# SSD mixer: transposed b in c b's bank, other places for a gate's three norms, three tiles in the first chunk of groups with 18, one tile in front of the first decays

## The chip, the cores and the metric

The kernel runs on one core of a Trainium2 chip. Its time is the device time of one execution in microseconds (us), the median of several runs. Before the change it is 2992.21 us (three runs, 2991.93 to 2997.83). Engines: PE multiplies matrices, DVE, ACT and POOL work on vectors, SP issues DMA transfers. Each takes its instructions in order and waits at an instruction until the work of other engines that it needs is done. Matmul results land in PSUM, memory of eight banks that PE writes and DVE and ACT read; everything else lies in SBUF.

## The reference, cut to what is touched

Two layers on 1040 tokens (16 meta tokens and 1024) of width 1024: a Mamba-2 mixer (SSD) with a gated convolution FFN, then stick-breaking attention with a second FFN. The change touches only the mixer, whose mathematics for each group of 8 heads is:

```python
z, xbc, dt_raw = jnp.split(u @ w_in, [SSM_D_INNER, SSM_D_INNER + SSM_CONV_DIM], axis=-1)
xbc = jax.nn.silu(_causal_dwconv(xbc, conv_w, conv_b))
xs, b_in, c_in = jnp.split(xbc, [SSM_D_INNER, SSM_D_INNER + G * N], axis=-1)
...
cb = jnp.einsum('bclgn,bcsgn->bgcls', c_c, b_c)
y_diag = jnp.einsum('bgcls,bgecls,bcsgep->bclgep', cb, decay_in, xdt)
chunk_states = jnp.einsum('bclgn,bgecl,bclgep->cbgepn', b_c, decay_to_end, xdt)
...
hg = (y * jax.nn.silu(z.astype(f32))).reshape(b, L, G, SSM_D_INNER // G)
hg = hg * lax.rsqrt(jnp.mean(hg * hg, axis=-1, keepdims=True) + NORM_EPS)
```

So each group has a projection with convolution and silu (x, B and C), a scan over chunks of tokens, a gate z, and a norm of the gated rows over the group's 512 channels.

## The kernel before

**Tiles.** Everything is kept transposed, channels on partitions, tokens along the row. A projected *tile* is 128 channels times a third of the tokens (348, 348, 344; the list TT). Each product is made of three matmuls in float32 halves (mm3, L171 to L173) over 8 blocks of the inner dimension, so 24 matmuls of one pass each per tile, into a PSUM bank `pj`.

**Streams of tiles.** `in_group(g)` makes 18 tiles: four rows of x, one of B, one of C, three thirds each. A tile is followed by its convolution (ACT L293, three operations of DVE L296) and, when the next tile is through, by a silu (ACT L484). `gate_group(g)` makes 12 tiles of z: silu (ACT L516), product with x (DVE L523), and, in `settle()` of the *next* tile, the square (ACT L528), which DVE adds to the third's accumulator (L532, L534). When a third has its four squares, `gate_norm(g, j)` can run: `rstd` loads an ACT table (L195), sums over partitions with a matmul by ones into a bank `ms` (PE L204), takes Ln and Exp on ACT (L207, L208), four steps on DVE (L209 to L212), then four products of DVE (L545) with the rows. `stream(blocks)` hands out all tiles one by one, in the order into(1), gate(0), into(2), gate(1), into(3), gate(2), gate(3). A block without a source stands for three calls (the norms), placed between tiles: in front of the second, third and fourth tile after the gate's last one, that is offsets 1, 2 and 3.

**Chunks.** The scan takes each group in 9 chunks of 116 tokens (the last 112; the list CH). A chunk has three parts. `ssd_decays`: SP fetches the cumulated decays, broadcast (D, L587, and E, L593), DVE subtracts (eight times, L598), ACT takes the exponential (L599), POOL multiplies E by C (L602). `ssd_front`: on PE the product cb (L614), four transpositions of x into px (L617), the transposed B into pb (L627); on DVE cb masked (cbm, L620), x times dt (xdt, L622), the decays times cbm (L623); ACT copies pb to bk (L629), POOL scales xdt to xde (L631). `ssd_back`: on PE the chunk's state S from bk and xde (L644), and y from the decays and the old state (L656, L658, 16 matmuls); POOL and DVE update the state (L650, L651), DVE adds y into x (L660, four times).

**What sets the order.** On PE, DVE, ACT and POOL the mixer's instructions stand in the order in which the program writes them. Between a chunk's front and its back stand tiles taken from the stream of the *next* groups, so that PE has work while DVE, ACT and POOL prepare S and y. The numbers of tiles that groups 0 to 3 spread over their chunks are (18, 30, 30, 18): two per chunk with 18, and 4, 3, 3 in turn with 30. The decays of the next chunk are issued to SP behind the first of a chunk's tiles, and their subtraction and exponential behind the second.

**Banks.** cb, pb, y and ms take turns in three PSUM banks (`sm`); px and S have two (`lg`); tiles have two for the first two thirds (`mm`) and one for the last (`ex`). A bank is free again when its readers are done.

Of the kernel before, what the change touches and what calls it, by code (L numbers as in the profile page):

```python
# [10 lines left out]
AF = mybir.ActivationFunctionType  # L11
ALU = mybir.AluOpType

P = 128
# [72 lines left out]
class Trunk:  # L87
# [465 lines left out]
    def stream(self, blocks, w0=None):  # L553


        calls = {}
        todo = []
        for src, f in blocks:
            if src is None:
                for j in range(3):  # L560
                    calls[3 * len(todo) + 1 + j] = lambda f=f, j=j: f(j)
            else:
                todo.append((src, f))
        w = [w0 or self.load_w(todo[0][0], D)]
        for n in range(3 * len(todo)):
            i, j = divmod(n, 3)
            if j == 0:
                if i + 1 < len(todo):
                    w.append(self.load_w(todo[i + 1][0], D))
                cur = w.pop(0)  # L570
            if n in calls:
                calls.pop(n)()
            todo[i][1](cur, j)
            yield
        self.settle()
        for f in calls.values():
            f()
# [27 lines left out]
    def ssd_front(self, g, x, bt, ct, c, dk, pool):  # L605

        nc = self.nc
        h0 = GH * g
        tt = nc.vector.tensor_tensor
        t0, n = CH[c]  # L610
        cc = 3 * (c % 3) + c // 3
        e = t0 + n
        pcb = self.sm("cb")
        nc.tensor.matmul(pcb[:n, :n], bt[:, t0:e], ct[:, t0:e], start=True, stop=True)  # L614
        px = self.lg("px")
        for q in range(4):
            nc.tensor.transpose(px[:n, q * P : q * P + P], x[q][:, t0:e], self.ident)  # L617
        px = px[:n].rearrange("p (h d) -> p h d", h=GH)
        cbm = pool.tile([P, CB], F32, tag="cbm", name=self.nm("cbm"), bufs=2)
        tt(cbm[:n, :n], pcb[:n, :n], self.past[:n, :n], op=ALU.mult)  # L620
        xdt = pool.tile([P, GH, 64], F32, tag="xdt", name=self.nm("xdt"), bufs=2)
        tt(xdt[:n], px, self.cols[:n, 0, cc, h0 : h0 + GH].unsqueeze(2).to_broadcast([n, GH, 64]), op=ALU.mult)  # L622
        tt(dk, dk, cbm[:n, :n].unsqueeze(1).to_broadcast([n, GH, n]), op=ALU.mult)  # L623
        bk = xde = None
        if c < 8:
            pb = self.sm("pb")
            nc.tensor.transpose(pb[:n, :P], bt[:, t0:e], self.ident)  # L627
            bk = pool.tile([P, P], F32, tag="bk", name=self.nm("bk"), bufs=2)
            nc.scalar.activation(bk[:n], pb[:n, :P], AF.Copy)  # L629
            xde = pool.tile([P, GH, 64], F32, tag="xde", name=self.nm("xde"), bufs=2)  # L630
            nc.gpsimd.tensor_tensor(xde[:n], xdt[:n], self.cols[:n, 2, cc, h0 : h0 + GH].unsqueeze(2).to_broadcast([n, GH, 64]), op=ALU.mult)  # L631
        return xdt, xde, bk
# [31 lines left out]
    def mixer(self, mx):  # L664
# [5 lines left out]
        with self.tc.tile_pool(name="ssd", bufs=3) as pool:  # L670
            yd, rows = [None] * 4, [[] for _ in range(4)]
            accs = [{} for _ in range(4)]
# [8 lines left out]
            def gate(g):  # L681
                def norm(j):
                    self.gate_norm(g, rows[g], accs[g], j)
                    if j == 2 and g < 2:
                        yd[g] = self.spill(rows[g][:4], f"y{g}_d")
                return self.gate_group(u, g, rows[g], accs[g], later if g == 3 else lambda j, f: f()) + [(None, norm)]

            into = lambda g: self.in_group(u, g, rows[g])
            blocks = into(1) + gate(0) + into(2) + gate(1) + into(3) + gate(2) + gate(3)
# [7 lines left out]
            with self.tc.manual_schedule(engines={E.PE, E.DVE, E.Activation, E.Pool}):  # L697
                ahead = self.ssd_decays(0, rows[0][5], 0, pool)
                dk, ce = next(ahead)
                for g in range(GROUPS):  # L700
                    *x, bt, ct = rows[g]
                    tiles, given = (18, 30, 30, 18)[g], 0
                    state = None
                    for c in range(9):
                        for _ in ahead:
                            pass
                        ops = self.ssd_front(g, x, bt, ct, c, dk, pool)
                        now = dk, ce
                        for _ in range((tiles * (c + 1) + 8) // 9 - given):
                            next(work)  # L710
                            if given == (tiles * c + 8) // 9:
                                nxt = (g, ct, c + 1) if c < 8 else (g + 1, rows[g + 1][5], 0) if g < 3 else None
                                ahead = self.ssd_decays(*nxt, pool) if nxt else iter([(None, None)])
                                dk, ce = next(ahead)
                            else:
                                next(ahead, None)
                            given += 1
                        state = self.ssd_back(g, x, c, *now, *ops, state, pool)
                        if g == 3:
                            done.append(c)  # L720
                            todo, waiting[:] = waiting[:], []
                            for w in todo:
                                later(*w)
# [909 lines left out]
```

## Time and profile before

| | us |
|---|---|
| median of three runs | 2992.21 |
| the profiled execution | 2995.8 |
| its span, first to last instruction | 2994.1 |
| mean granted clock of PE in it | 0.983 |
| PE busy from 285 to 380 us (group 1's last six chunks, two norms among them) | 89.07 of 95 |
| PE busy from 440 to 540 us (the same in group 2) | 94.10 of 100 |
| PE busy from 620 to 760 us (group 3's end, what follows) | 129.30 of 140 |

A line of the timeline or of a line's instructions reads: start in us, duration in us, engine, line of the program, operation, output, inputs, shapes, how many in a row, and in brackets the idle time of the engine just before with what ended it. A duration of several instructions in a row is that of all of them. PE's matmuls are pipelined, so that one tile's 24 matmuls start some 0.16 us apart though each is shown with 0.3 us. The window row of the profile lists start and end, its length, then for PE, the weight load, DVE, ACT and POOL the busy time with the number of instructions, then the granted clock, the share of the DMA engines, and GB/s.

### The profile page before, as it was taken

The page shows a single profiled execution, that of the slowest core. Times are in us where ns is not written, and L with a number is a line of the kernel's source. Part 1 is how long each engine was busy: PE and PEld are TensorE (multiplying, and loading weights), DVE is VectorE, ACT ScalarE, POOL GpSimd, SP SyncE. Part 2 cuts the span into 40 slices and gives each one's busy share as a digit, 9 for nine tenths or more (in the row PEclk, how much of TensorE's full clock was granted, in tenths as well). Part 3 has the DMA queues.
Part 4 walks back from the last instruction along what each step waited for, and adds up shares of the span by engine and source line. Part 5 has one row for each costly group of instructions (what it writes and reads, how often), then busy time and mean ns, then how long its engine had stood idle before and what let it go on. Part 6 is the DMA issues. An engine that isn't in the chain of part 4 may idle for free.

```text
span 2994.1 us, 57318 instructions
## 1 busy us (share of the span) xinstructions
PE 2879.0 (96%) x21863; PEld 2738.0 (91%) x21863; DVE 2304.0 (77%) x4026; ACT 1653.4 (55%) x3403; POOL 1308.0 (44%) x1250
## 2 busy tenths in 40 slices
PE   7999999989998999999999999999899999999998
PEld 4999898879998999998999999999798999998878
DVE  5586868885369887878876888888839878878785
ACT  4555555553245555555334788887736555554433
POOL 1254444442334666663442222222342766764451
PEclk9999999999999999999999999999999999999999
DMA  5233333323122222224232122221331222225321
GB/s 162 70 107 90 106 89 105 106 70 139 63 80 72 79 73 84 79 86 177 74 130 86 55 61 66 64 70 54 106 141 57 80 84 78 75 82 176 106 99 64
DMA packets 123411, 272.72 MB, mean 91 GB/s; under 512 B 13664, under 2 KB 53216, under 8 KB 123136
## 3 DMA queue, kind: packets, MB, share of 16 engines
q1 hardware_dynamic: 117760, 257.93, 26.6%
q10 hardware_dynamic: 4112, 6.56, 0.7%
q0 software_dynamic: 1264, 4.57, 0.4%
q8 instruction: 172, 2.82, 0.4%
q14 instruction: 103, 0.84, 0.1%
HBM read 200.89 MB, written 53.20 MB: 85 GB/s over the span
## 4 chain that ended last, share of the span: by engine, by line
PE 77%; DVE 12%; issue 4%; ACT 3%; POOL 2%; DMA 2%; SPq 0%; DVEq 0%; ACTq 0%; POOLq 0%
PE p L172 9%; PE p L171 9%; PE p L173 9%; PE acc L172 6%; PE acc L171 6%; PE acc L173 6%; PE pj L171 6%; PE pj L172 6%; PE pj L173 6%; PE po L1366 3%; PE lg L1325 3%; PE wT L1352 2%; DVE D L598 1%; PE ms L831 1%; DVE xbc L545 1%
## 5 line engine op out<-in xcount | busy, mean ns | idle before, releaser
L171 PE MATMUL pj<-uh,wh 128*128 128x348 f32 (+2 forms) x1536 | 507.0, 330 | 11.7 <-ACT bk L629 5.9
L172 PE MATMUL pj<-ul,wh 128*128 128x348 f32 (+2 forms) x1536 | 499.7, 325 | 0.0
L173 PE MATMUL pj<-uh,wl 128*128 128x348 f32 (+2 forms) x1536 | 496.3, 323 | 0.0
L171 PE MATMUL p<-bh,fh 128*128 128x262 f32 (+1 forms) x1408 | 403.5, 287 | 7.7 <-ACT c L293 2.8
L173 PE MATMUL p<-bh,fl 128*128 128x262 f32 (+1 forms) x1408 | 402.6, 286 | 3.6 <-POOL fl L905 3.6
L172 PE MATMUL p<-bl,fh 128*128 128x262 f32 (+1 forms) x1408 | 402.3, 286 | 0.1
L905 POOL TENSOR_TENSOR fl<-x,fh 128x1024 fp32r<-128x1024 f32 x88 | 212.4, 2414 | 267.4 <-ACT fh L904 217.7
L172 PE MATMUL p<-bl,wh 128*128 128x262 f32 (+1 forms) x1056 | 302.0, 286 | 6.1 <-DVE bl L857 6.1
L171 PEld LDWEIGHTS pj<-uh,wh 128*128 128x128 f32 x1536 | 292.8, 191 | 16.2 <-ACT xbc L293 4.3
L171 PE MATMUL p<-bh,wh 128*128 128x262 f32 (+1 forms) x1056 | 302.8, 287 | 0.9 <-ACT bh L856 0.9
L173 PE MATMUL p<-bh,wl 128*128 128x262 f32 (+1 forms) x1056 | 301.9, 286 | 0.0
L165 POOL TENSOR_TENSOR wl<-w,wh 128x1024 fp32r<-128x1024 f32 (+2 forms) x76 | 155.7, 2050 | 318.7 <-ACT wh L164 318.7
L172 PEld LDWEIGHTS pj<-ul,wh 128*128 128x128 f32 x1536 | 293.2, 191 | 1.8 <-issue 1.0
L173 PEld LDWEIGHTS pj<-uh,wl 128*128 128x128 f32 x1536 | 292.7, 191 | 0.8 <-issue 0.8
L296 DVE SCALAR_TENSOR_TENSOR c<-p,params,c 128x260 f32<-128x260 f32 (+1 forms) x528 | 249.8, 481 | 54.6 <-ACT c L293 45.1
L171 PEld LDWEIGHTS p<-bh,fh 128*128 128x128 f32 x1408 | 270.2, 192 | 8.6 <-ACT c L293 6.0
L173 PEld LDWEIGHTS p<-bh,fl 128*128 128x128 f32 x1408 | 269.4, 192 | 4.1 <-POOL fl L905 4.0
L172 PEld LDWEIGHTS p<-bl,fh 128*128 128x128 f32 x1408 | 270.2, 192 | 0.6 <-DVE bl L857 0.5
L947 DVE TENSOR_TENSOR c<-c,c 128x260 f32<-128x260 f32 (+1 forms) x176 | 245.0, 1394 | 5.5 <-ACT c L943 2.4
L952 ACT ACTIVATE ft<-p 128x262 f32<-128x262 f32 (+1 forms) x352 | 127.4, 384 | 203.8 <-DVE p L955 177.0
L1055 POOL TENSOR_TENSOR wl<-w,wh 128x1024 fp32r<-128x1024 f32 x56 | 148.9, 2662 | 205.4 <-ACT wh L1054 195.7
L171 PE MATMUL acc<-gh,wh 128*128 128x260 f32 (+1 forms) x672 | 215.0, 323 | 10.9 <-DVE h L1105 7.2
(325 smaller groups left out, 8472.7 us busy)
## 6 DMA issues: line engine op xcount, KB each, us to landing
w<-in_w_up SPq DMA_DIRECT2D x88, 512.0 KB
w<-in_w_down SPq DMA_DIRECT2D x44, 512.0 KB
w<-in_w_in SPq DMA_DIRECT2D x40, 512.0 KB
E<-ea_d SPq DMA_DIRECT2D x32, 464.0 KB
D<-acs_d SPq DMA_DIRECT2D x32, 420.5 KB
g<-c SPq DMA_DIRECT2D x88, 130.0 KB
g<-c SPq DMA_DIRECT2D x88, 128.0 KB
b<-g SPq DMA_DIRECT2D x16, 520.0 KB
```

The costliest lines, as they stand in the source:

```text
L165: nc.gpsimd.tensor_tensor(wl[:, :n], w32[:, :n], wh[:, :n].bitcast(F32), op=ALU.subtract)
L171: mm(out, wh, uh, start=first, stop=False, skip_group_check=joins)
L172: mm(out, wh, ul, start=False, stop=False, skip_group_check=joins)
L173: mm(out, wl, uh, start=False, stop=last, skip_group_check=joins)
L296: nc.vector.scalar_tensor_tensor(out, ps[:, o + i : o + i + n], wcol(i), out, op0=ALU.mult, op1=ALU.add)
L905: tt(lo[:, :n], t, hi[:, :n].bitcast(F32), op=ALU.subtract)
L947: self.last_up = tt(g[:, :FN], g[:, :FN], v[:, :FN], op=ALU.mult)
L952: nc.scalar.activation(s[:, :N], ps[:, :N], AF.Copy)
L1055: pt(wl, y, wh.bitcast(F32), op=SUB)
L1325: nc.tensor.matmul(ps[:nt, :m], part[:, c0 : c0 + nt], ks[a][:, s0 : s0 + m], start=x == 0, stop=x == 1)
L1352: nc.tensor.transpose(pt[:ns, x * CB : x * CB + nt], bt[a][:nt, x * CB : x * CB + ns], self.ident[:nt, :nt])
L1366: nc.tensor.matmul(po[64 * a : 64 * a + 64, :nt], v[: CH[c][1], c, 64 * a : 64 * a + 64], wt[a][: CH[c][1], c, :nt], start=x == 0, stop=x ...
```

## The change

Four things. (1) The transposed B goes to columns 128 to 255 of cb's bank, and is made ahead of cb; pb and its bank are gone. (2) The three norms of the gates of groups 0, 1 and 2 stand at the offsets -1, 1 and 3 from the gate's end instead of 1, 2 and 3: the first in front of the gate's last tile, the second where the first stood, the third where it was. Group 3's gate keeps 1, 2, 3. (3) In groups with 18 tiles the first chunk takes three tiles, and the others two up to the last, which takes one. (4) One tile is taken from the stream ahead of group 0's first decays; it counts as the first of that chunk's three. A flag `begun` takes the place of the old test for the next chunk's decays.

```diff
@@ stream
-            if src is None:
+            if isinstance(src, tuple):
                 for j in range(3):
-                    calls[3 * len(todo) + 1 + j] = lambda f=f, j=j: f(j)
+                    calls[3 * len(todo) + src[j]] = lambda f=f, j=j: f(j)
@@ ssd_front
         pcb = self.sm("cb")
+        if c < 8:
+            nc.tensor.transpose(pcb[:n, P : 2 * P], bt[:, t0:e], self.ident)
         nc.tensor.matmul(pcb[:n, :n], bt[:, t0:e], ct[:, t0:e], start=True, stop=True)
...
-            pb = self.sm("pb")
-            nc.tensor.transpose(pb[:n, :P], bt[:, t0:e], self.ident)
             bk = pool.tile([P, P], F32, tag="bk", name=self.nm("bk"), bufs=2)
-            nc.scalar.activation(bk[:n], pb[:n, :P], AF.Copy)
+            nc.scalar.activation(bk[:n], pcb[:n, P : 2 * P], AF.Copy)
@@ mixer
-                return self.gate_group(u, g, rows[g], accs[g], later if g == 3 else lambda j, f: f()) + [(None, norm)]
+                return self.gate_group(u, g, rows[g], accs[g], later if g == 3 else lambda j, f: f()) + [((-1, 1, 3) if g < 3 else (1, 2, 3), norm)]
...
                     for c in range(9):
+                        if g == c == 0:
+                            next(work)
+                            given = 1
                         for _ in ahead:
                             pass
+                        begun = False
                         ops = self.ssd_front(g, x, bt, ct, c, dk, pool)
                         now = dk, ce
-                        for _ in range((tiles * (c + 1) + 8) // 9 - given):
+                        for _ in range(min(tiles, (tiles * (c + 1) + 8) // 9 + (tiles == 18)) - given):
                             next(work)
-                            if given == (tiles * c + 8) // 9:
+                            if not begun:
+                                begun = True
                                 nxt = (g, ct, c + 1) if c < 8 else (g + 1, rows[g + 1][5], 0) if g < 3 else None
                                 ahead = self.ssd_decays(*nxt, pool) if nxt else iter([(None, None)])
                                 dk, ce = next(ahead)
```

In the changed program the lines from L614 to L625 have moved by one or two (cb is L616, its transposition L615, cbm L622, xdt L624, the product with cbm L625); L629, L644 and the others named above are the same.

PE around the first norm of the gate in group 1's chunks: `pj` are tiles, `ms` the norms' banks, `wh` and `wl` the halves of a weight block; what stands in brackets are the engines waited for. Before, the gate's last tile (344 tokens) follows the one ahead of it, and the first norm comes after a first tile of 352 columns:

```order
L173 MATMUL pj_2770<-uh_149,wl_2538 128x348
L171 MATMUL pj_2804<-uh_135,wh_2537 128x344 [waits Activation_49]
...
L173 MATMUL pj_2850<-uh_149,wl_2692 128x352
L204 MATMUL ms_2883<-z_2316,ones 128x348 [waits DVE_49]
L171 MATMUL pj_2896<-uh_135,wh_2691 128x352 [waits Activation_49]
```

and now:

```order
L173 MATMUL pj_2758<-uh_149,wl_2528 128x348
L204 MATMUL ms_2793<-z_2307,ones 128x348 [waits DVE_49]
L171 MATMUL pj_2806<-uh_135,wh_2527 128x344 [waits Activation_49]
...
L204 MATMUL ms_2885<-z_2340,ones 128x348 [waits DVE_49,PE_49]
L171 MATMUL pj_2898<-uh_135,wh_2680 128x352 [waits Activation_49]
```

The first norm's ms (of z_2307 now, z_2316 before: the same accumulator) stands ahead of the tile of 344 tokens, and where it stood is the second norm's.

DVE at the same place, now: `xbc_888` is a row of x that the gate multiplies, `z` a tile of the gate or its square, `cbm`, `xdt` and `D` those of the next chunk's front.

```order
L523 TENSOR_TENSOR xbc_888<-xbc_888,z_2709 128x348
L651 TENSOR_TENSOR state_2717<-state_2717,S_2715 128x512 [waits PE_49,Pool_49]
L660 SCALAR_TENSOR_TENSOR xbc_1184<-xbc_1184,params,y_2720 128x116 [waits PE_49]
...
L622 TENSOR_TENSOR cbm_2749<-cb_2741,past 116x116 [waits PE_49]
L624 TENSOR_TENSOR xdt_2751<-px_2744,cols 116x512 [waits PE_49]
L625 TENSOR_TENSOR D_2635<-D_2635,cbm_2749 116x928 [waits DVE_49]
L534 TENSOR_TENSOR z_2307<-z_2307,z_2709 128x348 [waits Activation_49]
L523 TENSOR_TENSOR xbc_888<-xbc_888,z_2783 128x348
L209 TENSOR_TENSOR z_2307<-y_2795 128x348 [waits PE_49,Activation_49]
```

The last addition to the first norm's accumulator (L534) stands behind the state, the four sums with y and the front of the next chunk, as it did before; the norm's own DVE steps (from L209) now follow two rows behind it.

ACT there, before (`bk` is the copy of the transposed B):

```order
L629 ACTIVATE bk_2766<-pb_2764 116x128 [waits PE_49]
L516 ACTIVATE z_2795<-pj_2770 128x348 [waits PE_49]
L528 ACTIVATE z_2720<-xbc_888 128x348 [waits DVE_49,Activation_49]
L516 ACTIVATE z_2829<-pj_2804 128x344 [waits PE_49]
```

and now:

```order
L629 ACTIVATE bk_2754<-cb_2741 116x128 [waits DVE_49]
L516 ACTIVATE z_2783<-pj_2758 128x348 [waits PE_49]
L528 ACTIVATE z_2709<-xbc_888 128x348 [waits Activation_49]
L195 ACT_TABLE_LOAD
L207 ACTIVATE y_2795<-ms_2793 128x348 [waits PE_49]
```

bk reads cb's bank and waits for DVE, which reads cb there, instead of PE.

DVE at the first decays, before:

```order
L296 SCALAR_TENSOR_TENSOR xbc_888<-pj_919,params,xbc_888 128x348 x3
L598 TENSOR_SCALAR D_1176<-D_1176,cols 116x116 x8
L296 SCALAR_TENSOR_TENSOR xbc_888<-pj_949,params,xbc_888 128x344 x3
L296 SCALAR_TENSOR_TENSOR xbc_985<-pj_986,params,xbc_985 128x348 x3
```

and now:

```order
L296 SCALAR_TENSOR_TENSOR xbc_1082<-pj_1143,params,xbc_1082 128x344 x3
L296 SCALAR_TENSOR_TENSOR xbc_1184<-pj_1185,params,xbc_1184 128x348 x3
L598 TENSOR_SCALAR D_1176<-D_1176,cols 116x116 x8
L622 TENSOR_TENSOR cbm_1231<-cb_1223,past 116x116
L624 TENSOR_TENSOR xdt_1233<-px_1226,cols 116x512
L625 TENSOR_TENSOR D_1176<-D_1176,cbm_1231 116x928
```

The convolutions of group 0's last tiles (xbc_888, xbc_985, xbc_1082) and of one tile of group 1 (xbc_1184) now stand ahead of the first decays' subtractions.

## The prediction

> **What bounds the kernel now.** I read the page first: its busy line, then the chain of waits by engine.
>
> ```profile
> PE 2879.0 (96%) x21863; PEld 2738.0 (91%) x21863; DVE 2304.0 (77%) x4026; ACT 1653.4 (55%) x3403; POOL 1308.0 (44%) x1250
> ...
> PE 77%; DVE 12%; issue 4%; ACT 3%; POOL 2%; DMA 2%; SPq 0%; DVEq 0%; ACTq 0%; POOLq 0%
> ```
>
> PE has work for 96% of the span, and the change neither adds nor removes a matmul (of the other engines' work only two table loads of ACT go, by the order). It can only give or take idle time of PE, and what the granted clock does behind it. All that it moves lies in the mixer, so the second view is PE's waits from 100 to 760 us (waiting work, releaser: us in all, times, longest):
>
> ```profile
> PE pb L627 <- DVE z L210: 6.8, 3, 2.6
> PE ms L204 <- ACT bk L629: 6.6, 3, 5.8
> PE pj L171 <- ACT bk L629: 5.9, 2, 3.0
> PE pj L171 <- DVE xbc L296: 4.0, 1, 4.0
> PE S L644 <- POOL xde L631: 3.0, 2, 2.3
> PE y L656 <- DVE D L623: 1.5, 1, 1.5
> ```
>
> They make 27.8 us, 0.9% of the program, and each row belongs to a part of the change: the first three stand around the gates' norms (pb waits for a bank that a norm still reads; bk, queued on ACT, then holds up what is behind it), the fourth at the first decays, the fifth at the first chunk of group 3, the sixth at its last. So the sum is small, and what counts is which waits come in their place.
>
> **1. A tile in front of the first decays.** From the timeline:
>
> ```profile
> 116.99 1.61 DVE L598 TENSOR_SCALAR D<-D,cols 116x116 f32<-116x116 f32 x8 [8.86 <-DMA D<-acs_d]
> 120.45 0.63 PE L171 MATMUL pj<-uh,wh 128*128 128x348 f32 x1 [4.03 <-DVE xbc L296]
> 120.88 0.49 PE L172 MATMUL pj<-ul,wh 128*128 128x348 f32 x1
> 121.17 0.49 PE L173 MATMUL pj<-uh,wl 128*128 128x348 f32 x1
> ...
> 125.50 0.32 PE L173 MATMUL pj<-uh,wl 128*128 128x348 f32 x1
> 125.66 0.32 PE L171 MATMUL pj<-uh,wh 128*128 128x348 f32 x1
> ```
>
> DVE works in order: L598 waits 8.86 us for the decays' DMA, the convs of finished tiles stand behind it, their PSUM banks stay taken, and PE stops for 4.03 us. Behind the stop the matmuls start 0.29 us apart (120.88 to 121.17) instead of 0.16 (125.50 to 125.66), for some 17 of them: 17 x 0.13 = 2.2 us. In the change the convs of group 0's last tiles and of one tile more are queued ahead of L598, so the banks come free while the DMA is under way. I take all of it, **-6.2 us**; the other end is nothing, where a later stage was short of time anyway (rival 3).
>
> **2. One tile instead of two in group 0's last chunk.** The nearest rows are those of the chunk before it:
>
> ```profile
> 216.30 0.46 PE L614 MATMUL cb<-xbc,xbc 128*116 128x116 f32 x2
> ...
> 220.37 1.11 DVE L623 TENSOR_TENSOR D<-D,cbm 116x928 f32<-116x928 f32 x1
> ...
> 227.42 3.88 DVE L598 TENSOR_SCALAR D<-D,cols 112x112 f32<-112x112 f32 x8
> ```
>
> y needs the product of the decays with cbm, which is done 220.37 + 1.11 - 216.30 = 5.2 us after cb starts. PE has the transpositions behind cb (about 0.7) and one tile, 24 matmuls x 0.16 = 3.8, so it is there at 4.5: **+0.7 us**. It is nothing if DVE comes sooner, and up to +4 if the subtractions of the last decays (3.88 us there) come in front and the clock falls behind the wait; the regular chunk is nearest, so 0.7.
>
> **3. Groups 1 and 2: norms at -1, 1 and 3, pb in cb's bank.** What the old places cost is read from the rows of S, one per chunk:
>
> ```profile
> 302.09 1.02 PE L644 MATMUL S<-xde,bk 116*128 116x512 f32 x2
> 323.34 1.02 PE L644 MATMUL S<-xde,bk 116*128 116x512 f32 x2
> 337.78 0.63 PE L171 MATMUL pj<-uh,wh 128*128 128x352 f32 x1 [3.01 <-ACT bk L629]
> 344.49 1.02 PE L644 MATMUL S<-xde,bk 116*128 116x512 f32 x2
> 363.47 1.02 PE L644 MATMUL S<-xde,bk 116*128 116x512 f32 x2
> 378.63 1.02 PE L644 MATMUL S<-xde,bk 116*128 116x512 f32 x2
> ...
> 459.75 1.02 PE L644 MATMUL S<-xde,bk 116*128 116x512 f32 x2
> 480.98 1.02 PE L644 MATMUL S<-xde,bk 116*128 116x512 f32 x2
> 499.55 1.13 PE L644 MATMUL S<-xde,bk 116*128 116x512 f32 x2
> ```
>
> An undisturbed chunk of three tiles takes 378.63 - 363.47 = 15.16, one of four 363.47 - 344.49 = 18.98; a tile is the difference, 3.82. In group 1 the two chunks with the norms have three tiles each and take 21.25 and 21.15: 21.25 - 15.16 less two ms pairs at 0.32 is 5.45, 21.15 - 15.16 is 5.99, together **11.4 us**. In group 2 the same two take 21.23 and 18.57: 5.43 + 3.41 = **8.8 us**. Of this I let all go: pb has no bank of its own to wait for, and the four products behind each norm (L545) no longer fall in the same chunk for two norms. The other end, that it all stays, is rival 2.
>
> What comes in its place: the first norm's ms now stands on PE in front of the gate's last tile, and its input gets its last square from the tile only two before, which ACT does behind the silu of the tile just finished, and which DVE adds behind everything that it has queued. Where the last tile starts in group 1 (290.05), the trace has these rows:
>
> ```profile
> 288.08 0.27 ACT L629 ACTIVATE bk<-pb 116x128 f32<-116x128 f32 x1
> 290.05 0.32 PE L171 MATMUL pj<-uh,wh 128*128 128x344 f32 x1
> 290.25 0.46 ACT L516 ACTIVATE z<-pj 128x348 f32<-128x348 f32 x1 [1.90 <-PE pj L173]
> 291.40 0.50 ACT L528 ACTIVATE z<-xbc 128x348 f32<-128x348 f32 x1 [0.69 <-DVE xbc L523]
> 292.24 0.69 DVE L651 TENSOR_TENSOR state<-state,S 128x512 f32<-128x512 f32 x1 [0.94 <-POOL state L650]
> 293.83 0.27 DVE L620 TENSOR_TENSOR cbm<-cb,past 116x116 f32<-116x116 f32 x1
> 294.61 1.12 DVE L623 TENSOR_TENSOR D<-D,cbm 116x928 f32<-116x928 f32 x1
> 295.64 1.37 DVE L534 TENSOR_TENSOR z<-z,z 128x348 f32<-128x348 f32 x1
> 297.64 0.75 PE L204 MATMUL ms<-z,ones 128*128 128x348 f32 x2
> ```
>
> The square is done at 291.9, but the add (L534) stands behind state, four sums of x, cbm, xdt and the product with cbm, and ends at 297.0. PE, in order, would stand still from 290.05 to 297.0, 7.0 us, with the last tile queued behind ms. The stop's clock: 2.2 us was lost behind the stop of 4.03, and at 337.78 the chunk's excess of 5.99 less the wait of 3.01 leaves 3.0; I take 2.5. With 0.5 for what arrives late afterwards that is 10.0 per gate: **-1.4 us** in group 1, **+1.2** in group 2, **-0.2** together. The least it can be is ACT's and DVE's own chain, 0.46 + 0.50 + 0.52 (an uncontended add) and gaps, some 2 us, if DVE's queue is empty (rival 1). The second norm stands where the first stood and its input is then one tile older than it needs, so it stops nothing.
>
> [...]
>
> Sharing a bank has its own price: bk (ACT) now waits until DVE has read cbm, at 293.83 + 0.27 = 294.1, where it ran at 288.08, and on ACT the silu of the tile just finished and the square stand behind it. Here that ends at 294.1 + 0.27 + 0.46 + 0.50 = 295.3, still ahead of the add at 295.64, so I cost it at nothing; in other chunks DVE's part of the held-up tile stands behind the product with cbm as well. Without that cover S, a tile of 3.82 or more behind, would wait for bk by at most 294.1 - 288.1 - 3.8 = 2.2 us per chunk.
>
> [...]
>
> **4. Group 3.** The third tile in the first chunk covers the wait of S there; what binds afterwards is POOL's and DVE's turn per chunk.
>
> ```profile
> 561.87 1.62 PE L644 MATMUL S<-xde,bk 116*128 116x512 f32 x2 [2.27 <-POOL xde L631]
> 569.17 1.79 POOL L631 TENSOR_TENSOR xde<-xdt,cols 116x512 f32<-116x512 f32 x1 [2.94 <-DVE xdt L622]
> 617.29 1.85 POOL L631 TENSOR_TENSOR xde<-xdt,cols 116x512 f32<-116x512 f32 x1 [4.34 <-DVE xdt L622]
> 642.58 1.53 PE L204 MATMUL ms<-z,ones 128*128 128x348 f32 x2 [5.83 <-ACT bk L629]
> ...
> 618.20:666.40 48.20, 38.48 (x276) 33.87 (x274) 41.71 (x85) 28.05 (x38) 22.38 (x12) 0.89 0.17 52
> ```
>
> From 569.17 to 617.29 four chunks take 48.12, 12.03 each, while PE needs 15.16 - 3.82 = 11.3 for two tiles. So PE gets ahead of DVE again, and the 2.27 comes back as later waits; between 0 and 2.3 us gain. From 618.2 to the last y DVE is busy 41.71 of 48.20 us (third number group of the window), with the same instructions after the change. At most 6.5 us can go there, the wait of 5.83 at 642.58 among it; against it stands a stop at the first norm as in groups 1 and 2. I take **0**, with -3 and +3 as ends.
>
> **Sum.** -6.2 + 0.7 - 0.2 + 0 = -5.7 us, against the profiled execution's 2995.8 us (span 2994.1 and 1.7 around it): 2990.1. That execution lies 3.6 us above the median of the runs shown, 2992.21, and the same step from the median gives 2986.5; I say 2986. The ends of the terms (±3 for group 3, +3 for part 2, ±2 for each gate's stop) make its own range 2982 to 2991.
>
> **Rivals.**
> 1. The first norm hardly stops PE, because DVE's queue is shorter there once the pile is gone. Then a stop of 2 us without loss of clock leaves 11.4 - 2.4 = 9.0 and 8.8 - 2.2 = 6.6, and the total is -5.7 + 0.2 - 15.6 = -21, **2971 us**. For it: the square is done at 291.9 and POOL's state, which delays DVE at 292.24, might come earlier. Against it: all of the chunk's front is ahead of L534 in DVE's order.
> 2. Slower. The stop comes on top of the old waits, in all three gates: DVE is behind by as much as the norm's own work, the pile is only moved by one tile, and the wait of bk for cbm takes the place of that of pb for its bank. Only pb's wait for its bank, 6.8 / 3 = 2.3 us per gate, is sure to go: 7.0 - 2.3 = +4.7 for each gate, +14.1 for three, less 5.5 for parts 1 and 2: +8.6, **3001 us**. The kernel is slower than before from 1.9 us per gate above what I have, 5.7 / 3. For it: pb's waits show that DVE is the late one. Against it: the second norm is a tile further from the third.
> 3. The gain of the first decays is eaten before the group ends: S(0) then waits for xde, since the subtractions come behind three convs. Then -1 in all, **2991 us**. Against it: the chunks of group 0 show no waits of PE afterwards.
>
> **Numbers.** The forecast has 0.55, rival 1 0.15, rival 2 0.18, rival 3 0.12. 0.2% is 6.0 us, about what a measurement of this kernel can tell from no change, so faster ends at 2986.2 and slower begins at 2998.2. The forecast lies on the first bound: half of it, 0.27, and rival 1 make faster 0.42. Of rival 2, which lies close to the other bound, I count 0.13 as slower, and 0.01 of the forecast: 0.14. The rest, 0.44, is the same. The range takes in the nearer half of rival 1 and of rival 2: 2970 to 3001, and leaves out some 0.16.
>
> **What would show it.** In the profile of the changed kernel: no wait of pj for L296 near 120 us and starts 0.16 us apart there (part 1, else rival 3). A row of ms L204 waiting for DVE L534 or ACT's square some 6 to 7 us in each of three gates (part 3; about 2 us speaks for rival 1). No wait for L210 (else rival 2), and chunks with 15.2 us where 21.2 stood. A wait of y for the product with cbm under 1 us at group 0's end. S at group 3's first chunk without a wait, and the last y within 3 us of its old distance from there. I would be wrong above all if DVE's order around the first norm does not hold, by the row that releases that ms.

## The result, and the profile after

The changed kernel takes 2993.6 us (median of 20 runs, 2986.8 to 2998.3) beside 2993.1 for the kernel before (20 runs): a ratio of 0.9998, 95% interval 0.9991 to 1.0005, that is -0.6 us with -2.7 and +1.5 as ends. (The means are 2993.2 with the change and 2993.7 before, the other way round than the medians.) Nothing was gained that can be measured. All ratios here are of undisturbed executions; one of e12's twelve, of 3586 us, is left out. The profiled execution took 2996.4 us, span 2994.7, mean granted clock 0.984.

The page's busy line and the chain by engine are nearly those of before:

```profile
PE 2876.7 (96%) x21863; PEld 2733.4 (91%) x21863; DVE 2295.3 (77%) x4026; ACT 1646.5 (55%) x3401; POOL 1303.6 (44%) x1250
...
PE 78%; DVE 12%; ACT 3%; issue 3%; DMA 2%; POOL 2%; ACTq 0%; SPq 0%; DVEq 0%; POOLq 0%
```

PE's waits from 100 to 760 us, however, have been exchanged for others:

```profile
PE ms L204 <- DVE z L534: 17.0, 5, 6.9
PE y L656 <- DVE D L625: 8.2, 1, 8.2
PE S L644 <- POOL xde L631: 5.0, 5, 1.4
PE pj L171 <- DVE xbc L296: 1.2, 2, 0.6
```

The waits at the first decays, of pb for L210 and behind bk are gone. In their place stand ms waiting for the last square's sum (L534), and 8.2 us in front of the last y. The four rows make 31.4 us, where the six of before made 27.8.

The start of the program drifts from execution to execution: the instruction named below starts at 100.73 us in e3 and at 103.94 in e1, 3.2 apart. So that places inside the mixer can be compared, all times below are counted from one instruction ahead of the first decays, a DVE step whose start the timelines of before and after give as

```profile
103.01 0.46 DVE L457 TENSOR_TENSOR cols<-end,cols 116x288 f32<-116x288 f32 x1 [1.15 <-ACT cd L456]
```

```profile
102.19 0.46 DVE L457 TENSOR_TENSOR cols<-end,cols 116x288 f32<-116x288 f32 x1 [1.15 <-ACT cd L456]
```

From it to the end of group 0 (the first S of group 1), from there to the S of group 1's chunk 7, to that of group 2, to the last y of group 3, and to the first matmul of the out-projection, each kernel's profiled execution is longer (+) or shorter (-) than that of before by so many us:

| kernel | group 0 | group 1 | group 2 | group 3 | to the out-projection | all |
|---|---|---|---|---|---|---|
| the change | -6.7 | +0.1 | +2.1 | +3.1 | +1.6 | +0.2 |
| e3 first decays only | -6.3 | -2.4 | +3.0 | -1.5 | 0.0 | -7.1 |
| e13 the same again | -6.3 | +0.5 | +1.8 | -1.4 | 0.0 | -5.4 |
| e4 norms only | -0.6 | +0.2 | +2.1 | -0.8 | +1.6 | +2.6 |
| e5 bank only | -0.1 | +0.5 | +1.7 | +0.8 | +2.7 | +5.7 |
| e1 the change, norms at 1, 2, 3 | -6.6 | +0.7 | +1.8 | +1.2 | +2.6 | -0.4 |
| e9 the change, third tile in group 0 only | -6.6 | 0.0 | +2.1 | +3.4 | +1.5 | +0.4 |
| e2 the change, norms at 1, 3, 5 | -6.7 | -0.4 | +1.5 | -0.9 | +2.4 | -4.1 |
| e8 as e1, without L545 in groups 0 and 1 | -6.7 | -6.4 | -4.1 | +2.6 | +1.6 | -13.0 |
| e10 first decays, norms at 1, 4, 6 | -6.3 | -0.5 | +1.3 | -0.1 | 0.0 | -5.6 |
| e11 first decays, ms copied | -6.3 | -0.1 | +2.2 | +0.4 | 0.0 | -3.7 |
| e12 as e11, products split | -6.3 | -0.9 | +1.5 | +0.8 | +1.6 | -3.4 |
| e14 first decays, norms at 1, 3, 5 | -6.3 | +2.6 | +5.1 | -6.8 | +1.6 | -3.8 |

e3 and e13 are the same program, and groups 1 and 2 in them are those of before. Their rows show how far two executions differ there: 3 us in a group. The last section shows the granted clock at one stop of group 1, 1.00 in e3 and 0.50 in e13; group 2 of the profiled execution of before was a fortunate one, so that +1.5 to +2 in that column is no price of any edit. Behind the first matmul of the out-projection all kernels are the same program, and still these executions take from 4.3 us less (e1) to 5.5 us more (e10) there than that of before. So a part is better judged by the table than by the time of a single run.

The first gain of the change, 6.7 us in group 0, is given back for the most part in group 3 and behind it, 4.7 us; groups 1 and 2 come out near nothing, the +2.1 of group 2 being that chance of before. In group 1 the rows of S and ms in the change are:

```profile
275.08 1.02 PE L644 MATMUL S<-xde,bk 116*128 116x512 f32 x2
289.52 1.53 PE L204 MATMUL ms<-z,ones 128*128 128x348 f32 x2 [6.93 <-DVE z L534]
305.07 1.02 PE L644 MATMUL S<-xde,bk 116*128 116x512 f32 x2
320.75 1.02 PE L644 MATMUL S<-xde,bk 116*128 116x512 f32 x2
336.96 1.12 PE L644 MATMUL S<-xde,bk 116*128 116x512 f32 x2
```

The chunk with the stop takes 29.99 us where an undisturbed one of four tiles takes 18.98 and two ms pairs 0.64: 10.4 us lost, 6.93 as the stop and 3.4 behind it. The next two, of three tiles, take 15.68 and 16.21 where 15.16 is undisturbed: 1.25 of the former 11.4 is left, beside the third norm's 0.32. What the stop waits for is on DVE and ACT (timeline of the change):

```profile
286.28 0.27 DVE L622 TENSOR_TENSOR cbm<-cb,past 116x116 f32<-116x116 f32 x1
...
286.59 0.28 ACT L629 ACTIVATE bk<-cb 116x128 f32<-116x128 f32 x1 [5.94 <-DVE cbm L622]
...
287.07 1.11 DVE L625 TENSOR_TENSOR D<-D,cbm 116x928 f32<-116x928 f32 x1
...
288.10 1.36 DVE L534 TENSOR_TENSOR z<-z,z 128x348 f32<-128x348 f32 x1
```

L534 comes behind the next chunk's cbm, xdt and product, as in the order, and bk waits 5.94 us on ACT for cbm. That wait is hidden here: ACT's square, at 287.10, still ends ahead of L534.

Group 3 in the change, from its second S to its last y:

```profile
570.11 1.13 PE L644 MATMUL S<-xde,bk 116*128 116x512 f32 x2 [1.00 <-POOL xde L631]
582.11 1.13 PE L644 MATMUL S<-xde,bk 116*128 116x512 f32 x2 [0.69 <-POOL xde L631]
594.84 1.12 PE L644 MATMUL S<-xde,bk 116*128 116x512 f32 x2 [1.37 <-POOL xde L631]
612.35 0.89 PE L204 MATMUL ms<-z,ones 128*128 128x348 f32 x2 [2.52 <-DVE z L534]
635.98 1.12 PE L644 MATMUL S<-xde,bk 116*128 116x512 f32 x2 [1.42 <-POOL xde L631]
648.48 1.12 PE L644 MATMUL S<-xde,bk 116*128 116x512 f32 x2 [0.56 <-POOL xde L631]
664.13 0.74 PE L656 MATMUL y<-D,xdt 112*64 112x112 f32 x4 [8.18 <-DVE D L625]
```

PE is ahead of POOL and DVE in nearly every chunk, and waits the largest piece at the end. The granted clock behind that last stop, from the window view (third number from the end):

```profile
664.13:666.13 2.00, 2.00 (x21) 2.00 (x23) 0.48 (x1) 1.39 (x2) 1.05 (x1) 0.50 0.00 0
666.13:668.13 2.00, 2.00 (x19) 1.72 (x16) 0.60 (x3) 0.00 (x0) 2.00 (x2) 0.62 0.00 0
```

PE runs at half clock, 0.50, for 3.5 us after it; half of that, as an estimate, is about the +1.6 of the column behind group 3.

### The profile page after: what moved, and what is told of

Its sections match the earlier page's. It is cut to its first block, busy times and chain, and to the rows that moved or that the text cites. A ratio compares the mean times of both kernels' runs of the same rounds, so it can differ in the third digit from the quotient of the medians.

```text
span 2994.7 us, 57311 instructions
## 1 busy us (share of the span) xinstructions
PE 2876.7 (96%) x21863; PEld 2733.4 (91%) x21863; DVE 2295.3 (77%) x4026; ACT 1646.5 (55%) x3401; POOL 1303.6 (44%) x1250
## 4 chain that ended last, share of the span: by engine, by line
PE 78%; DVE 12%; ACT 3%; issue 3%; DMA 2%; POOL 2%; ACTq 0%; SPq 0%; DVEq 0%; POOLq 0%
PE p L173 9%; PE p L172 9%; PE p L171 9%; PE acc L172 7%; PE acc L171 7%; PE acc L173 7%; PE pj L171 6%; PE pj L172 6%; PE pj L173 6%; PE po L1371 3%; PE lg L1330 3%; PE wT L1357 2%; DVE D L598 1%; PE ms L836 1%; DVE xbc L545 1%
```

## The experiments

Two questions stood: whether places of norms, the bank or DVE's amount of work makes the loss in groups 1 and 2, and what ate the first decays' gain in group 3.

**e1, the norms back at 1, 2, 3** (rest of the change kept; 12 runs):

```diff
-                return self.gate_group(...) + [((-1, 1, 3) if g < 3 else (1, 2, 3), norm)]
+                return self.gate_group(...) + [((1, 2, 3), norm)]
```

> The change with the norms of all gates back at 1, 2 and 3; bank, third tile and the tile in front of the first decays stay. Theory A (the first norm's new place costs 10.4 us in each of groups 1 and 2, and the bank alone would have taken the old waits away): no wait of ms for L534 over 1 us in groups 1 and 2, no wait for L210, S of group 1's chunk 7 some 11 us earlier than before beyond the 7.5 of group 0, the same in group 2 some 8 us, in all 15 to 19 us below the change. Rival B (the old waits come from DVE's pile of two norms in one chunk, the bank is only where they show): the wait for L210 moves to another instruction, the stop of 3 us at a tile behind bk stays, and group 1 gains at most 5 us; in all 0 to 10 us below the change.

Measured: 2992.5 us, ratio to before 1.0004 (0.9993 to 1.0015). Rival B: the shared bank did not take the old waits away.

**e5, the bank alone** (before, with the transposed B in cb's bank; a single run):

```diff
+        if c < 8:
+            nc.tensor.transpose(pcb[:n, P : 2 * P], bt[:, t0:e], self.ident)
...
-            pb = self.sm("pb")
-            nc.tensor.transpose(pb[:n, :P], bt[:, t0:e], self.ident)
...
-            nc.scalar.activation(bk[:n], pb[:n, :P], AF.Copy)
+            nc.scalar.activation(bk[:n], pcb[:n, P : 2 * P], AF.Copy)
```

> The kernel before with only the transposed B in cb's bank. Theory A: the waits of pb for L210 and of tiles behind bk go in groups 1 and 2, 9 to 11 us each, and group 3 is as before within 2 us. Rival B: 0 to 5 us each. Rival C on group 3 (bk's wait for cbm is what made group 3 some 5 us slower in the change): group 3 is 3 to 5 us longer than before here, with waits of S or of tiles behind bk.

Measured: 3000.7 us in one run, above all 23 runs of before shown beside it (2986.2 to 2999.2). PE's waits from 230 to 540 us, groups 1 and 2, first before, then with the bank shared:

```profile
PE pj L171 <- ACT bk L629: 5.9, 2, 3.0
PE pb L627 <- DVE z L210: 5.1, 2, 2.6
PE ms L204 <- ACT bk L629: 0.7, 2, 0.4
```

```profile
PE pj L171 <- DVE xbc L296: 7.5, 4, 3.2
PE ms L204 <- DVE z L210: 5.1, 2, 2.6
PE ms L204 <- DVE xbc L660: 2.3, 2, 1.9
```

The wait for L210 is the same 5.1 us to the tenth, but it is now the second norm's ms that waits: it is the next to take a bank whose last reader is the first norm's L210. Taking pb out of the rotation hands the wait to its successor. The stop of 3 us at a tile is there too, released by DVE instead of bk. In group 3 the last y now has a stop of its own,

```profile
669.04 0.74 PE L656 MATMUL y<-D,xdt 112*64 112x112 f32 x4 [6.60 <-DVE D L625]
```

where before had 1.48: the stop of 5.83 in the middle of the group (2.49 now) has gone to its end, and behind it 2.7 us are lost up to the out-projection. DVE itself is hardly later: the last y starts 133.3 us after the start of group 3, beside 132.5 in before.

**e4, the norms alone** (before, with the norms at -1, 1, 3; a single run):

```diff
-                return self.gate_group(...) + [(None, norm)]
+                return self.gate_group(...) + [((-1, 1, 3) if g < 3 else (1, 2, 3), norm)]
```

> The kernel before with only the norms of groups 0 to 2 at -1, 1 and 3. Counted from the same event ahead of the mixer's chunks, theory D (DVE's own load in the chunks with the norms sets the loss, so places only move it): stops of ms for L534 of 6 to 7 us in groups 1 and 2, no wait of pb for L210, groups 1 and 2 longer by 0 to 4 us together, group 3 longer by 1 to 4; in all 1 to 8 us slower. The theory of the prediction (the wait for pb's bank is a price of its own that the shared bank had to remove): the waits of pb for L210 stay beside the new stops, 2 to 3 us per gate, and the kernel is 8 us slower or more.

Measured: 2996.5 us in one run, +2.6 in the table. Groups 1 and 2 with the norms alone, and with the whole change:

```profile
PE ms L204 <- DVE z L534: 13.6, 2, 6.8
PE pj L171 <- ACT bk L629: 1.0, 2, 0.5
```

```profile
PE ms L204 <- DVE z L534: 13.8, 2, 6.9
PE pj L171 <- DVE xbc L296: 1.2, 2, 0.6
```

No wait for L210 is left although pb still has its own bank. It is the distance of the norms that removes the old waits, not the bank; the two add nothing to each other. In all three kernels and in before the two groups' waits are 12 to 15 us.

**e8, without the products of the norms** (as e1, without L545 in groups 0 and 1, so that the rows of these groups go out unscaled; a single run):

```diff
-        for q in range(4):
+        for q in range(0 if g < 2 else 4):
             xq = x[q][:, s0 : s0 + n]
             self.nc.vector.scalar_tensor_tensor(xq, xq, self.par("gate_norm", 4 * g + q), r, op0=ALU.mult, op1=ALU.mult)
```

> The change with the norms at 1, 2, 3, and without the four products of each norm (L545) for groups 0 and 1, so that these groups' rows are not scaled. Theory D: the waits in groups 1 and 2 (8.2 and 6.3 us there with the products) go for the most part, under 2.5 us left in each, and with the clock 6 to 11 us in group 1 and 5 to 9 in group 2. If instead banks or bk's place on ACT hold PE, the waits stay within 1.5 us of those.

Measured: 2978.9 us in one run. Groups 1 and 2 against e1: -6.4 - 0.7 = -7.1 and -4.1 - 1.8 = -5.9 us. Their waits:

```profile
PE ms L204 <- DVE z L210: 5.1, 2, 2.6
PE pj L171 <- DVE xbc L296: 1.0, 2, 0.8
PE cb L616 <- ACT xbc L484: 1.0, 1, 1.0
```

The third row lies in group 3 already, whose first chunk stands before 540 us here. So of 14.9 us in e1 6.1 are left, all but 1 of it the bank's wait for L210; what went are the stops at tiles and at ms behind DVE. The sizes are as theory D has them, though group 1 with 3.4 us of rest is above the 2.5 per group that it allowed. So with the norms at 1, 2, 3 their products on DVE make somewhat more than half of the waits, 8.8 us, and the bank's late reader a steady 2.5 per gate.

**e2, the norms at 1, 3, 5** (the change otherwise; 11 runs), **e10 at 1, 4, 6** in groups 0 and 1 and **e14 at 1, 3, 5** (the last two on before with the first decays' tile, e10 a single run, e14 12 runs). The edits of e2 and e10:

```diff
-                return self.gate_group(...) + [((-1, 1, 3) if g < 3 else (1, 2, 3), norm)]
+                return self.gate_group(...) + [((1, 3, 5) if g < 3 else (1, 2, 3), norm)]
```

```diff
-                return self.gate_group(...) + [(None, norm)]
+                return self.gate_group(...) + [((1, 4, 6) if g < 2 else (1, 2, 3), norm)]
```

> The change with the norms of groups 0 to 2 at 1, 3 and 5: as far apart as in the change, but none in front of a tile of its own gate. Theory A: no stop at the first norm (its input is as old as before the change), and with two tiles between norms no pile: 18 to 22 us below the change, all of it in groups 1 and 2 (11 and 9) and 2 in group 3. Rival B agrees on the first norm but has the pile moved one tile later, with 3 to 5 us of waits left per gate: 8 to 14 us below the change. A third possibility, that norms two tiles later hold the rows and banks longer and stop the next group's tiles, would show as waits of pj for L545 or L210.

> The kernel before with the tile in front of the first decays (group 0 alone), and the norms of groups 0 and 1 at 1, 4 and 6, one in each of three chunks; bank and group 3 as before. By theory D a norm costs little where no other stands in its chunk: groups 1 and 2 each 3 to 7 us shorter than before, 10 to 18 us in all with the 7 of the first decays. If each norm's block of DVE work stops PE by itself wherever it stands, groups 1 and 2 are within 2 us of before, 7 us in all.

> The kernel before with the tile in front of the first decays (group 0 alone) and the norms of groups 0 to 2 at 1, 3 and 5; bank and the tiles of group 3 as before. The pieces say: -6.3 to -6.6 up to the end of group 0, groups 1 and 2 between 2 us shorter and 2 longer (as with these offsets and the shared bank), group 3 within 2 of before: 5 to 9 us below the kernel before, ratio 0.997 to 0.998. If the spread norms only paid with the shared bank, groups 1 and 2 are 3 us or more longer and little of the 6 is left.

Measured: e2 2990.0 us, ratio 0.9993 (0.9984 to 1.0002); e10 2995.9 in one run (-5.6 in the table; 5.5 us were lost again behind the mixer, where the program is the same); e14 2991.7, ratio 0.9995 (0.9984 to 1.0007). The 8 to 22 us that e2 and e10 were to bring are nowhere, nor are the 5 to 9 of e14. In groups 1 and 2 of e2 the one releaser left is the tile's convolution:

```profile
PE pj L171 <- DVE xbc L296: 14.6, 12, 2.2
```

Twelve short stops make the sum of two long ones. In e10 the first two norms of a gate each bring a wait of pb (the third brings none), and in e14 the third norm's ms waits once for long:

```profile
302.20 0.32 PE L627 MATMUL pb<-ident,xbc 128*116 128x128 f32 x1 [2.56 <-DVE z L210]
322.54 0.32 PE L627 MATMUL pb<-ident,xbc 128*116 128x128 f32 x1 [2.85 <-DVE z L210]
```

```profile
325.89 1.52 PE L204 MATMUL ms<-z,ones 128*128 128x344 f32 x2 [8.21 <-ACT bk L629]
```

Wherever the norms stood, PE waited 12 to 22 us in the two groups (12.5 in e10, 21.5 in e14). e14 and e2 differ in the bank, in group 3's tiles and in nothing else; with pb's bank these offsets do worse in groups 1 and 2 and better in group 3. The -6.8 there is the largest gain in that column; a kernel with these offsets for group 2's gate alone, whose norms fall in group 3, was not run.

**e3 and e13, the first decays' tile alone** (the same program, e3 a single run, e13 11 runs; before with one tile in front of group 0's first decays, three tiles in its chunk 0 and one in chunk 8):

```diff
+                        if g == c == 0:
+                            next(work)
+                            given = 1
...
-                        for _ in range((tiles * (c + 1) + 8) // 9 - given):
+                        for _ in range(min(tiles, (tiles * (c + 1) + 8) // 9 + (g == 0)) - given):
...
```

> The kernel before with only the tile in front of group 0's first decays (and so three tiles in chunk 0 and one in chunk 8 of group 0). If the gain of the first decays is real and kept, S of group 1's chunk 0 stands 7.5 us earlier than before, and everything up to the end of the mixer as well, since groups 1 to 3 are then as they were: 7 us less at the out-projection. If group 3 gives no time away because DVE binds it by absolute time, the end of the mixer moves by less than 4.

> The first decays' tile alone once more, now timed: 7 us below the kernel before by the first look's trace (ratio 0.9976), if the first look's gain is the part's own; within 2 us of it if it was that one execution's.

Measured: e3 2986.9 in one run, e13 2988.2 us (11 runs), ratio 0.9986 (0.9977 to 0.9996): 4.2 us, between 1.2 and 6.9, faster than before, and the one version whose interval lies clearly off 1. That is between the 7 us that e3's trace promised and the 2 us that would have made it one execution's chance. 6.3 us is gained by the end of group 0, and at the out-projection 7.1 (e3) and 5.4 us (e13) are there. Three rows of group 3 in e13:

```profile
632.18 0.32 PE L627 MATMUL pb<-ident,xbc 128*116 128x128 f32 x1 [1.79 <-DVE z L210]
638.33 1.53 PE L204 MATMUL ms<-z,ones 128*128 128x348 f32 x2 [5.83 <-ACT bk L629]
661.56 0.42 PE L656 MATMUL y<-D,xdt 112*64 112x112 f32 x3 [1.48 <-DVE D L623]
```

These are the waits of before, to the hundredth but for one. Group 3 does not eat a lead that comes from ahead of it. What ate it in the change was done to group 3 itself.

**e9, the third tile in group 0 only** (a single run):

```diff
-                        for _ in range(min(tiles, (tiles * (c + 1) + 8) // 9 + (tiles == 18)) - given):
+                        for _ in range(min(tiles, (tiles * (c + 1) + 8) // 9 + (g == 0)) - given):
```

> The change with the third tile only in group 0's first chunk; group 3 has two tiles there and two in its last again. Theory E (DVE and POOL set group 3's pace, and the third tile only puts DVE's part of the second chunk later): from S of group 2's chunk 7 to the last y group 3 is 2 to 3 us shorter than in the change, and the stop before that y is 3 to 5 us instead of 8.2, as one more tile stands there. If the third tile is a gain as it was meant, group 3 is 2 us longer instead, with the wait of S in its first chunk back at 1.5 us or more.

Measured: 2993.7 in one run; group 3 and what follows +3.4 + 1.5 = +4.9, beside +4.7 in the change. The stop before the last y,

```profile
664.65 0.75 PE L656 MATMUL y<-D,xdt 112*64 112x112 f32 x4 [4.56 <-DVE D L625]
```

is shorter than 8.18 by 3.62, nearly the tile of 3.82 that stands in front of it again. So neither side was right: the third tile in group 3 neither pays nor costs, as far as one execution tells. The last y comes when DVE has its product, and a tile more or less ahead of it only fills the stop.

**e11 and e12, DVE's reader taken from the bank, and products moved** (both with the first decays' tile, 12 runs each). In e11 ACT copies the norm's sum out of its bank, so that DVE need not read it there; e12 has that too, and hands two of the four products to POOL and ACT in the first two norms of groups 0 and 1:

```diff
+        if keep:
+            nc.scalar.activation(b[:, :n], ps[:, :n], AF.Copy)
         nc.scalar.activation(y, y, AF.Exp, scale=-0.5)
...
+        if keep:
+            nc.vector.tensor_tensor(b[:, :n], b[:, :n], y, op=ALU.mult)
+            nc.vector.tensor_tensor(b[:, :n], b[:, :n], y, op=ALU.mult)
...
```

```diff
+            if g < 2 and q < 2 and j < 2:
+                self.nc.gpsimd.tensor_tensor(xq, xq, r, op=ALU.mult)
+                self.open.append(lambda xq=xq, q=q: self.nc.scalar.activation(xq, xq, AF.Copy, scale=self.par("gate_norm", 4 * g + q)))
...
```

> The kernel before with the tile in front of the first decays, and in each gate's norm ACT copies the norm's sum from its bank to SBUF right behind Ln, so that DVE (two products with y in place of L209 and L210) no longer reads the bank. If the wait for L210 is only the bank of the first norm's ms held by DVE's late reader, whichever instruction takes that bank next, the waits for L210 (6.8 us in three gates) go, and 7 to 14 us in all with the first decays' 7, so 2979 to 2985. If DVE's load alone sets the pace there, PE waits as long at the next thing that DVE owes, a tile bank behind L296 or behind bk, and the kernel gains 5 to 8 in all.

> The same, and in the first two norms of groups 0 and 1 two of the four products run on POOL (by r) and ACT (by the gain, with the next tile's settling) instead of DVE. By theory D, DVE's block per norm gets 1.0 us shorter by its own duration, and groups 1 and 2 gain 1 to 4 us each over the kernel without it. If DVE's stretching beside POOL's work (L545 at 4.21 instead of 2.06 for four, L598 at 4.04 instead of 1.60 for eight) is the larger part, more work on POOL gives it back: 0 or up to 5 us slower.

Measured: e11 2989.6 us, ratio 0.9988 (0.9977 to 0.9999), no better than e13; e12 2991.1, ratio 0.9995 (0.9983 to 1.0008), so that less work on DVE and more on POOL and ACT brought nothing. In e11 no wait for the norm's reader is left, and PE stops as long at the norm's ms behind bk (first row); in e12 both stops of group 1 have become one there (second fence):

```profile
301.25 1.42 PE L204 MATMUL ms<-z,ones 128*128 128x348 f32 x2 [2.56 <-ACT bk L635]
331.70 0.40 PE L171 MATMUL pj<-uh,wh 128*128 128x352 f32 x1 [3.23 <-ACT bk L635]
```

```profile
305.98 1.53 PE L204 MATMUL ms<-z,ones 128*128 128x348 f32 x2 [6.27 <-ACT bk L639]
```

A bank freed earlier, and two of four products moved away, changed where PE waits and hardly how long: 13.9 us in groups 1 and 2 in e11 and 13.8 in e12, beside 12.5 in e13.

## Why the prediction was right, and where it was not

The forecast was a gain of 6 us at the edge of what can be told from no change, with 0.44 for no change. The time, 2993.6, lies in the range of 2970 to 3001, but 2.6 us above the forecast's own range of 2982 to 2991; rival 3 (2991) comes nearest in size, not in its mechanism. That the time lies in the range is owed to the upper part of it, taken in for rival 2, and not to the forecast's own sum; two of its terms, the bank and group 3, were off, while the first decays and the sizes in groups 1 and 2 were right. (Rival 1's price counts its stop of 2 us as 2.4 in one group and 2.2 in the other and gives no reason; nothing hangs on it.) By its terms:

- **First decays, -6.2.** Right. The first S of group 0 comes 2.7 us earlier with 3.82 of a tile more ahead of it: 6.5 us, and e3 and e13 show the gain kept to the out-projection. Rival 3, that S(0) of the same group eats it, is refuted.
- **One tile in group 0's chunk 8, +0.7.** No row for y's wait there, and group 0 ends with -6.7: the term was nothing.
- **The first norm's stop, 7.0, and 10.0 with its clock.** 6.93 and 6.88 in groups 1 and 2, and 10.4 in all in group 1. Rival 1 asked for 2 us and is refuted; DVE's order decided it, as read from the rows before.
- **The old waits, 11.4 and 8.8, go.** They do: 1.25 is left in group 1. But the reason was half wrong. The prediction gave pb's bank a share; e4 and e5 show that the spacing alone removes them and the bank alone does not. Group 1's -1.4 measured +0.1. In group 2, +1.2 forecast and +2.1 measured: that the old price was smaller there is the clock's chance and no property of the group: behind the stop at that place, 2.94 us in before and 3.21 in e13, the clock stays at 1.00 in before (windows from 490 to 500 us) and falls to 0.50 in e13 (492.79 to 494.79).
- **Sharing the bank, 0.** This is a step that failed. The prediction costed it where bk's longer wait is hidden, in group 1, and it is hidden there. e5 has it at +0.8 in group 3 and +2.7 behind it. The timed runs agree: e1 is e13 with the bank shared and a third tile in group 3, and their ratios, 1.0004 and 0.9986, differ by 0.0018, 5.4 us; the intervals just overlap, and e9 has the third tile at nothing.
- **Group 3, 0 with -3 and +3.** This is the term that decided: +3.1 to the last y and +1.6 behind it, 4.7, outside its ends; against e13's group 3 (-1.4 and 0.0), which starts with nearly the same lead and has none of the edits, 6.1. The mechanism named there, DVE and POOL set the group's pace, is right: PE waits for them in most chunks. What was missing is what follows from it. PE's gained time collects in one stop before the last y: 4.6 to 8.3 us in the six profiles with the bank shared, 1.5 to 2.4 in the eight without. The clock behind that stop, 0.50, then goes with up to 2.7 us more (e5). The bank adds to both columns (e5: +0.8 and +2.7). The +1.6 of e4 need be no price of the norms' places: e11 and e12 have the same stop of 2.31 us before the last y, and 0.0 and +1.6 behind it. From the start of group 3 the last y comes 4.4 us later in the change than in e13, and 2.6 of them are there with the norms back at 1, 2, 3 (e1). Which of DVE's steps in the last chunks makes them was not settled.

Rival 2 had the right place for half of its story: alone, the shared bank leaves the waits where they were under another name. In the change it did not come to the sum of old and new waits, since the spacing removes the old ones.

In groups 1 and 2 then the change swaps waits of much the same size, 11.7 us before and 15.0 after. e8 shows what they are made of with the norms at 1, 2, 3: somewhat more than half is DVE's products for the norms. That it is so for the other places too is likely, since the waits stay there, but no run shows it.

## What to carry to other kernels

When an engine that feeds the bottleneck has too much work in a few chunks, moving a step among those chunks, or giving a bank back sooner, can move the wait to the next instruction that needs that engine, as it did here (11.7 us in groups 1 and 2 before, 12 to 22 wherever the norms stood); look for the sum of waits over the stage, not for the one that has a name. A lead is worth having only where nothing else sets the pace: 6.3 us gained where a DMA was waited for was kept, and the edits of the DVE-bound last group lost as much. Try the parts of a change singly: here one part paid 4 us, and the version with that part alone has the lowest ratio of those that were run several times, though its interval overlaps that of others.

## What the runs showed of the chip

At one place of the program a stop of about 3 us went with a granted clock of 0.50 in one execution and of 1.00 in another. Behind the stop of 3.01 us at 337.78 in before, and behind that of 3.03 us in e3 at the same place of the program, at 329.17, the windows give (clock third from the end):

```profile
337.78:339.78 2.00, 2.00 (x7) 2.00 (x8) 2.00 (x7) 2.00 (x4) 0.00 (x0) 0.50 0.21 85
341.78:343.78 2.00, 2.00 (x8) 2.00 (x7) 1.93 (x4) 0.99 (x2) 2.00 (x2) 0.50 0.00 0
```

```profile
329.17:331.17 2.00, 2.00 (x12) 2.00 (x13) 2.00 (x7) 2.00 (x4) 0.00 (x0) 1.00 0.20 83
333.17:335.17 2.00, 1.90 (x17) 1.03 (x18) 1.93 (x4) 0.98 (x2) 2.00 (x2) 1.00 0.03 8
```

Some 3 us go with it, by the difference between e3 and e13 in group 1 (-2.4 and +0.5): in e13, behind the stop of 3.24 at that place, the clock is 0.50 in the windows from 332.72 to 336.72. In before, whose group 2 looked cheap, it is 1.00 behind the stop of 2.94 at 495.34. After the long stop in the change the clock is low for 6 us:

```profile
289.50:291.50 2.00, 1.98 (x5) 1.50 (x6) 0.40 (x1) 0.42 (x1) 0.00 (x0) 0.50 0.00 0
...
293.50:295.50 2.00, 2.00 (x9) 2.00 (x8) 1.93 (x5) 0.00 (x0) 0.00 (x0) 0.50 0.00 0
295.50:297.50 2.00, 2.00 (x14) 2.00 (x13) 0.70 (x2) 0.54 (x2) 0.00 (x0) 0.98 0.00 0
```

Narrow windows give both ends of a stretch with the clock at 0.50. From 96 to 776 us before has six, from 118.63 to 125.46, 309.78 to 313.19, 337.08 to 343.91, 466.79 to 470.20, 562.36 to 565.78 and 637.46 to 647.70, and the change four, from 285.35 to 295.59, 442.36 to 452.60, 613.03 to 616.44 and 660.82 to 667.64. Each of the ten lasts 3.41, 6.83 or 10.24 us (four, three and three of them). In before 2.31 of the 3.01 us of the stop lie ahead of 337.08, where a low stretch starts. What makes the clock fall there in before and not in e3 was not shown.

What was lost behind three of the stops is near half of what was left of the stretch when the stop ended; that it is the half is an estimate from the 0.50. In the stretch at the long stop in the change 6.1 us lie behind the stop: 3.0 us, where 10.4 - 6.93 = 3.4 were lost. In the one at the last y of the change it is 3.5 us, and +1.6 was lost; in e5 the clock is 0.50 from the stop's end to near 674.97 (0.52 in the window from 673.04 to 675.04), 5.9 us, and +2.7 was lost.

The slow starts behind 120.45 in before, 0.29 us apart, lie in the stretch from 118.63 to 125.46.
